# Linear attention's level products: each head alone on 64 rows, in two tiles of the scores' pool

## The chip, the cores and the metric

The kernel runs on one core of a Trainium2 chip. A core has five engines that work side by side, each through a queue of its own: TensorE (PE, matrix products into PSUM; its weight loads are listed as PEld), VectorE (DVE), ScalarE (ACT), GpSimd (POOL) and SyncE (SP, which issues the DMAs). The metric is the device time of one execution in microseconds, the median over runs.

## The reference

One step of a one-layer decoder. A 2048-token prompt and a small batch of 8 x 8 sample tokens go through an RMS norm and one input projection, whose columns feed two mixers: dilated sliding-window attention (8 heads of 64) and gated linear attention (GLA, 4 heads with key dimension 64 and value dimension 128). Both are gated, concatenated, projected and added to the input. What the change touches is GLA's scores within a chunk:

```python
b = jnp.cumsum(gc, axis=2)
diff = b[:, :, :, None, :] - b[:, :, None, :, :]
decay = jnp.exp(jnp.where(causal[:, :, None], diff, -jnp.inf))
scores = jnp.einsum('bhtk,bhsk,bhtsk->bhts', qc, kc, decay)
o = (jnp.einsum('bhts,bhsv->bhtv', scores, vc)
     + jnp.einsum('bhtk,bhkv->bhtv', qc * jnp.exp(b), state))
```

The score of query t with key s is a sum over 64 key dimensions, each with its own decay exp(b_t - b_s), for s not after t, separately for each head h.

## The kernel before

**Levels.** The decay has a factor per key dimension, so the scores aren't one matrix product. The kernel builds the lower triangle from levels. At level B (1, 2, 4, ..., 64) the tokens are cut into blocks of B; within each pair of blocks the left one gives keys and the right one queries, and the decay is split at the block border: exp(b_t - b_m) on the query, exp(b_m - b_s) on the key, both at most 1. One product per level then gives the scores of all such pairs, and a mask picks the part that belongs to them. The diagonal is set apart. A `gla_core` object works on 256 tokens (two chunks of 128): eight such objects (e0 to e7) for the prompt, and one small one (smp, three levels) for the samples.

**Where heads lie.** Keys and queries are turned so that the key dimension lies on the 128 partitions: a pair p of heads (two of the four) shares them, head j = 0 on partitions 0 to 63 and j = 1 on 64 to 127. Pairs and tokens lie along the row.

**`front(li)`** prepares a level. POOL subtracts the border's b (L236, tile D). ACT takes the exponential into E in three instructions (L244): the keys' half for all partitions into E[0], the queries' half of partitions 0 to 63 into E[1], and of 64 to 127 into E[2]. The other halves of E[1] and E[2] stay zero from a fill at the start (the loop at L1246, memset at L1252). DVE multiplies the keys into ks (L249, 128x256) and the queries into qbd (L252, 128x512): both blocks of qbd hold the same queries, but one has zeros on partitions 64 to 127, the other on 0 to 63. So a product over all 128 partitions gives two heads side by side with nothing of the one in the other.

**`back(li)`** makes the scores. A tile of the scores' pool ps_S (two buffers of one PSUM bank each) takes the products (L281): for each chunk c, head pair p and half k0 of the chunk's keys, one of 128 contracted partitions, 64 key columns as weights and 2 x 32 queries. That makes 8 products a level; each fp32 product runs as two passes, so the profile counts 16 matmuls. The first half of the keys goes to partitions 0 to 63 of the scores, the second to 64 to 127. DVE then copies the masked part into Ac (L287, copy_predicated). Level 64 (L267) has only keys of the first half: 4 products of 2 x 64 queries, all on partitions 0 to 63, copied by ACT into `full` (L273). `filled` copies Ac into `full` (L302).

**Order.** `gla_prompt` runs steps s = 0 to 8 for each core object e: front(s), then back(s - 2); `turned` and the two chunks of e - 1 at s = 0, 1 and 2 (`chunk`: U at L1275, the products with state and scores at L1283 and L1289, the state update Sbd at L1296 on DVE, the output copy on ACT); the next object's loads at s = 3, its `turn` and `decay` at 5 and 6. `weave` deals these steps out between the steps of the host, the input projections of g, vb and gb (L1127; 24 fp16 matmuls per 128 tokens and block, evicted by ACT), and beside them the weight preparation (`load_w`: ACT and DVE at L649 and L650), the dot products of the sample attention (`late_dots`: POOL at L1515, DVE at L970) and the sample's own linear attention (`sample_gla`). Each engine executes its instructions in the order in which they stand in its queue. That order is mostly the source's, but a planner lays it out with a timeline of its own and can put an instruction that is ready ahead of an earlier one that isn't.

After this stage the output projection follows (L1658), with the sample attention beside it.

Of the kernel before, what the change touches and what calls it, by code (L numbers as in the profile page):

```python
# [7 lines left out]
F32 = mybir.dt.float32  # L8
# [3 lines left out]
I32 = mybir.dt.int32  # L12
# [6 lines left out]
P = 128  # L19
# [33 lines left out]
def tile_hymba(ctx: ExitStack, tc: tile.TileContext, A: dict):  # L53
# [89 lines left out]
    class gla_core:  # L143
# [19 lines left out]
        def turn(self):  # L163
# [65 lines left out]
        def front(self, li):  # L229
            gt, st, n, B = self.pools[1], self.st, self.n, self.levels[li]  # L230
            halves = lambda f: f.rearrange("p (m two B) -> p m two B", two=2, B=B)
            M = n // B
            bv = halves(self.b[:].rearrange("p a c -> p (a c)"))
            D = gt.tile([P, 2 * n], F32, name=f"D_{self.tagp}_{B}", tag="D", bufs=2)
            dv = halves(D[:])
            dec = POOL.tensor_tensor(  # L236
                dv, bv, bv[:, :, 0:1, B - 1 : B].to_broadcast([P, M, 2, B]), ALU.subtract
            )
            E = st["E"][li % 2]
            ev = E[:, :, :n].rearrange("p i (m B) -> p i m B", B=B)  # L240
            for i, (rows, half) in enumerate(
                ((slice(0, P), 0), (slice(0, 64), 1), (slice(64, P), 1))
            ):
                ACT.activation(  # L244
                    ev[rows, i], dv[rows, :, half, :], AF.Exp, scale=(2 * half - 1) / 16.0
                )
            ks, qbd = st["ks"][li % 3], st["qbd"][li % 3]
            kv, qv = (halves(f.rearrange("p a c -> p (a c)")) for f in (self.kT, self.qT))
            DVE.tensor_tensor(  # L249
                halves(ks[:, : 2 * n])[:, :, 0, :], kv[:, :, 0, :], ev[:, 0], ALU.mult  # L250
            )
            que = DVE.tensor_tensor(  # L252
                qbd[:, :, :n].rearrange("p i (m B) -> p i m B", B=B),
                qv[:, :, 1, :].unsqueeze(1).to_broadcast([P, 2, M, B]), ev[:, 1:3], ALU.mult,
            )
            st["pins"] = (dec.ins, que.ins)

        def back(self, li):
            st, n, C, nch, B = self.st, self.n, self.C, self.nch, self.levels[li]
            ps_s, Ac = self.pools[3], self.Ac  # L260
            ks, qbd = st["ks"][li % 3], st["qbd"][li % 3]
            sc = ps_s.tile([P, 512], F32, name=f"sc_{self.tagp}_{B}", tag="S")
            if B == 64:

                for c in range(nch):
                    for p in range(2):
                        PE.matmul(  # L267
                            sc[:64, (c * 2 + p) * P : (c * 2 + p + 1) * P],
                            ks[:, p * n + c * C : p * n + c * C + 64],
                            qbd[:, :, (p * nch + c) * 64 : (p * nch + c + 1) * 64],  # L270
                            start=True, stop=True,
                        )
                ACT.activation(  # L273
                    self.full[0:64, :, 64:], sc[:64].rearrange("p (g t) -> p g t", t=64), AF.Copy
                )
                return
            for c in range(nch):
                for p in range(2):
                    o = (c * 2 + p) * 64
                    for k0 in range(0, C, 64):  # L280
                        PE.matmul(  # L281
                            sc[k0 : k0 + 64, o : o + 64],
                            ks[:, p * n + c * C + k0 : p * n + c * C + k0 + 64],
                            qbd[:, :, p * (n // 2) + (c * C + k0) // 2 :][:, :, :32],
                            start=True, stop=True,
                        )
            DVE.copy_predicated(  # L287
                Ac[:C].rearrange("p g (m two B) -> p g m two B", two=2, B=B)[:, :, :, 1, :],
                self.mask[:C, li].bitcast(I32).unsqueeze(1)
                .to_broadcast([C, nch * 4, 32]).rearrange("p g (m B) -> p g m B", B=B),  # L290
                sc[:C, : nch * 128].rearrange("p (g m B) -> p g m B", g=nch * 4, B=B),
            )
# [89 lines left out]
    with ExitStack() as c1:  # L382
# [862 lines left out]
        st = {"wgu": wgu, "E": [], "ks": [], "qbd": []}  # L1245
        for lst, nm_, shape, m, eng in (  # L1246
            (st["E"], "E", [P, 3, 256], 2, DVE), (st["ks"], "ks", [P, 512], 3, DVE),
            (st["qbd"], "qbd", [P, 2, 256], 3, DVE), (Sbd, "Sbd", [P, 2, 256], 2, POOL),
        ):
            for i in range(m):  # L1250
                t = gst.tile(shape, F32, name=f"{nm_}{i}")
                eng.memset(t[:], 0.0)  # L1252
# [14 lines left out]
        def chunk(core, gc):  # L1267
# [13 lines left out]
            for p in range(2):  # L1281
# [5 lines left out]
                for j in range(2):  # L1287
                    h = 2 * p + j
                    PE.matmul(  # L1289
                        O[:, h * P : (h + 1) * P], full[:, c * 4 + h, :],  # L1290
# [74 lines left out]
        def sample_gla():  # L1365
            while "dots" not in mixed:
# [13 lines left out]
            E, ks, qbd = (  # L1380
                own[:, 0:192].rearrange("p (i c) -> p i c", i=3), own[:, 192:320],
                own[:, 320:448].rearrange("p (i c) -> p i c", i=2),
            )
            own = {"wgu": wgu, "E": [E] * 2, "ks": [ks] * 3, "qbd": [qbd] * 3}
# [27 lines left out]
            for p in range(2):  # L1412
                O = ps_O.tile([P, 512], F32, name=f"O_s{p}", tag="O")
                for j in range(2):
# [8 lines left out]
                    for bt in range(8):  # L1423
# [5 lines left out]
                        O[:NS, j * P : (j + 1) * P], Am[:NS, h, :],  # L1429
# [606 lines left out]
```

## Time and profile before

| what | us |
|---|---|
| median of 3 runs | 1332.17 (1331.6 to 1335.26) |
| the profiled execution | 1337.86 |
| its span in the profile | 1336.1 |
| PE busy in the span | 1219.8 (91%) |
| DVE busy | 919.4 (69%) |
| ACT busy | 877.0 (66%) |
| POOL busy | 631.5 (47%) |
| mean granted TensorE clock | 0.974 |

The first level product of the prompt's linear attention starts at 744.6 us of the span, the last at 1022.2. All durations quoted below are from the one profiled execution. PE's busy time has modelled ends: a matmul's length contains the latency of the array, so the cost of a matmul in a stream is read from the distance of starts.

### The profile page before, as it was taken

What the parts mean: (1) busy time and instruction counts of PE and PEld (TensorE: products, weight loads), DVE (VectorE), ACT (ScalarE), POOL (GpSimd) and SP (SyncE); (2) the same over time, 40 slices, a digit from 0 to 9 for tenths busy, and PEclk for the clock granted to TensorE, in tenths of its full rate; (3) what the DMA queues carried; (4) which work ended last, traced back from release to release, by engine and by line L of the source; (5) the groups of instructions that cost most, each with busy time, mean ns of one, the idle gap of its engine ahead of it and who ended that gap; (6) DMA issues with size and microseconds to landing.
All of it is one profiled execution on the core that took longest, in us unless ns stands there. A gap on an engine that the chain in (4) does not pass through costs nothing.

```text
span 1336.1 us, 26268 instructions
## 1 busy us (share of the span) xinstructions
PE 1219.8 (91%) x8910; PEld 732.2 (55%) x8910; DVE 919.4 (69%) x2271; ACT 877.0 (66%) x2332; POOL 631.5 (47%) x596
## 2 busy tenths in 40 slices
PE   3797999989889898998999899999999989999998
PEld 1333565555555555676777566666655445444443
DVE  6357667788767876776765988777672388787741
ACT  5645787777668875878897667665774475565610
POOL 0067545678678745561113965665452144232310
PEclk9989999999999899999899999999999989999999
DMA  8859967777875599969886556553334788998952
GB/s 257 248 152 238 223 198 159 195 209 229 206 201 172 156 265 274 319 218 225 194 210 179 183 165 210 167 167 119 108 101 158 256 253 288 363 344 324 334 194 79
DMA packets 251800, 285.27 MB, mean 214 GB/s; under 512 B 125441, under 2 KB 160338, under 8 KB 251666
## 3 DMA queue, kind: packets, MB, share of 16 engines
q1 hardware_dynamic: 251666, 283.60, 70.7%
q8 instruction: 70, 1.15, 0.4%
q14 instruction: 64, 0.52, 0.1%
HBM read 183.12 MB, written 75.24 MB: 193 GB/s over the span
## 4 chain that ended last, share of the span: by engine, by line
PE 35%; DVE 19%; DMA 16%; issue 11%; ACT 9%; POOL 9%; SPq 2%; POOLq 0%; DVEq 0%; ACTq 0%
PE Y L1658 6%; PE acc_vb L1127 3%; DVE qbd L252 3%; PE acc_gb L1127 3%; PE acc_qkb L1127 3%; PE acc_g L1127 3%; POOL pr L965 2%; PE t L462 2%; PE O L477 2%; DMA T_q<-qp_d 2%; PE s L444 2%; DVE p L452 2%; DVE sck L970 2%; POOL pt L429 2%; DVE ks L249 1%
## 5 line engine op out<-in xcount | busy, mean ns | idle before, releaser
L1127 PEld LDWEIGHTS <-hr 128*128 128x128 f16 x1824 | 174.0, 99 | 133.9 <-issue 16.0
L1127 PEld LDWEIGHTS <-hl 128*128 128x128 f16 x1248 | 122.7, 100 | 154.9 <-issue 28.8
L455 ACT ACTIVATE p<-p,o 128x256 f32<-128x256 f32 (+1 forms) x384 | 173.3, 455 | 47.0 <-DVE o L452 39.8
L1658 PE MATMUL Y<-w_o,mh 128*128 128x512 f16 x768 | 178.0, 383 | 6.7 <-ACT mh L1617 6.6
L965 POOL TENSOR_TENSOR pr<-k,qb 128x512 f32<-128x512 f32 x96 | 132.5, 1380 | 91.8 <-DVE sck L970 58.6
L429 POOL TENSOR_TENSOR pt<-p,pt 128x512 f16<-128x512 f32 (+1 forms) x80 | 94.2, 1178 | 156.3 <-ACT pt L428 125.9
L477 PE MATMUL O<-v,pt 128*128 128x128 f16 x1200 | 113.1, 223 | 22.1 <-POOL pt L429 9.7
L1658 PEld LDWEIGHTS <-mh 128*128 128x128 f16 x768 | 71.9, 98 | 94.3 <-issue 9.0
L970 DVE TENSOR_REDUCE sck<-pr 128x8 f32<-128x512 f32 x128 | 85.6, 678 | 48.9 <-POOL pr L965 48.7
L462 PE MATMUL t<-ident,p 128*128 128x128 f32 x600 | 108.8, 286 | 7.3 <-ACT p L455 5.7
L477 PEld LDWEIGHTS <-pt 128*128 128x128 f16 x1200 | 83.7, 100 | 47.5 <-POOL pt L429 14.3
L1127 PE MATMUL acc_v<-w_v,hl 128*128 128x512 f16 x384 | 96.5, 396 | 8.8 <-DVE vp L759 3.1
L1127 PE MATMUL acc_g<-w_g,hr 128*128 128x272 f16 (+1 forms) x768 | 102.9, 280 | 0.0
L452 DVE CUSTOM_DVE_ANT_0 p<-s,m3w,scl_s 128x128 f32<-128x128 f32 (+1 forms) x256 | 89.0, 394 | 15.9 <-PE s L444 5.7
L1700 POOL TENSOR_TENSOR tc<-oc,w 128x512 f32<-128x512 f32 x32 | 47.0, 1490 | 111.7 <-DVE w L1692 104.8
L1127 PE MATMUL acc_q<-w_q,hl 128*128 128x512 f16 x384 | 93.8, 394 | 4.6 <-ACT zs_k L677 3.8
L244 ACT ACTIVATE E<-D_e 128x256 f32<-128x256 f32 x168 | 66.2, 417 | 43.8 <-POOL D_e L236 26.2
L1127 PE MATMUL acc_k<-w_k,hl 128*128 128x512 f16 x384 | 90.4, 381 | 3.1 <-ACT zs_k L677 2.6
L1127 PE MATMUL acc_vb<-w_vb,hr 128*128 128x512 f16 x384 | 89.1, 379 | 2.3 <-ACT zg L733 2.3
L444 PE MATMUL s<-kk,qq 128*128 128x256 f16 (+1 forms) x512 | 82.4, 273 | 8.9 <-DMA kk<-kp_d 5.2
L1127 PE MATMUL acc_gb<-w_gb,hr 128*128 128x512 f16 x384 | 87.7, 381 | 0.0
L462 PEld LDWEIGHTS t<-ident,p 128*128 128x128 f32 x600 | 70.3, 146 | 18.1 <-ACT p L455 11.3
(509 smaller groups left out, 2630.4 us busy)
## 6 DMA issues: line engine op xcount, KB each, us to landing
k<-in_cache_k_win SPq DMA_DIRECT2D x104, 256.0 KB
sv<-in_cache_v_win SPq DMA_DIRECT2D x24, 1024.0 KB
hr<-h_d SPq DMA_DIRECT2D x44, 512.0 KB
qb<-q_d SPq DMA_DIRECT2D x64, 256.0 KB
o_d<-o SPq DMA_DIRECT2D x96, 132.0 KB
oc<-o_d SPq DMA_DIRECT2D x48, 264.0 KB
x<-in_x_prompt SPq DMA_DIRECT2D x16, 512.0 KB
h_d<-hl SPq DMA_DIRECT2D x16, 512.0 KB
```

Source lines behind the costliest of these rows:

```text
L244: ACT.activation(ev[rows, i], dv[rows, :, half, :], AF.Exp, scale=(2 * half - 1) / 16.0)
L429: POOL.tensor_tensor(l, f, h, ALU.subtract)
L444: PE.matmul(s_ps[:, i * w : (i + 1) * w], q, k, start=(n == 0), stop=(n == len(prods) - 1),)
L452: DVE.tensor_tensor_reduce(s[:, sl], s_ps[:, sl], mask, neg, BIG, ALU.add, ALU.min, nmf(i))
L455: ACT.activation(s[:, sl], s[:, sl], AF.Exp, bias=nmf(i), scale=-1.0, accum_out=denf(i))
L462: PE.transpose(p_ps[:, i * P : (i + 1) * P], t["s"][:, i * P : (i + 1) * P], ident[:])
L477: PE.matmul(o_, t["pt"][:, c, (i * nb + b) * P : (i * nb + b + 1) * P], vf(i, b), start=(n == 0), stop=(n == 2 * nb - 1),)
L965: POOL.tensor_tensor(pr[:], kt, qt, ALU.mult)
L970: DVE.tensor_reduce(out, pr[:].rearrange("p (u k d) -> p u k d", u=2, k=4), AX.X, ALU.add)
L1127: PE.matmul(z, a_[:, k, :], w[:, p_, k, cols], start=(k == 0 and i == 0), stop=(k == KT - 1 and i == 2),)
L1658: PE.matmul(Y[:], a_[:, k, :], w_[:, part, k, :512], start=(i == 0), stop=(i == len(prods) - 1),)
L1700: eng.tensor_tensor(t_[:], oc[:, g, :, 0:64], w[:, g].unsqueeze(2).to_broadcast([P, NH, HD]), ALU.mult,)
```

## The change

The level products are made for each head alone. The queries qs are 128x256 with no zero blocks (E has two parts, and ACT takes the queries' exponential in one instruction). Each product contracts the 64 partitions of one head, and its result goes to a tile of that head's place j: `sc` is now two tiles of ps_S, so a level takes both buffers of the pool. There are 16 products of 32 queries a level (32 matmuls in the profile's count) and 8 of 64 at level 64. The masked copy into Ac and the copy of level 64 into `full` run once per tile. The heads in Ac and `full` are now ordered (j, c, p), in place of (c, p, j), which the diagonal (POOL) and the readers of `full` and Ac follow. Fills of E and of the queries are dropped.

```diff
 in turn():
+            g = nch * 2
             POOL.tensor_tensor(
-                Ac[:C],
-                ident64[:C].unsqueeze(1).to_broadcast([C, nch * 4, 64]),
-                dd[:C].unsqueeze(2).to_broadcast([C, nch * 4, 64]),
+                Ac[:C].rearrange("p (j g) t -> p j g t", j=2),
+                ident64[:C].unsqueeze(1).unsqueeze(1).to_broadcast([C, 2, g, 64]),
+                dd[:C].rearrange("p (g j) -> p j g", j=2).unsqueeze(3).to_broadcast([C, 2, g, 64]),
                 ALU.mult,
             )
 in front():
-            for i, (rows, half) in enumerate(
-                ((slice(0, P), 0), (slice(0, 64), 1), (slice(64, P), 1))
-            ):
+            for half in range(2):
                 ACT.activation(
-                    ev[rows, i], dv[rows, :, half, :], AF.Exp, scale=(2 * half - 1) / 16.0
+                    ev[:, half], dv[:, :, half, :], AF.Exp, scale=(2 * half - 1) / 16.0
                 )
...
             que = DVE.tensor_tensor(
-                qbd[:, :, :n].rearrange("p i (m B) -> p i m B", B=B),
-                qv[:, :, 1, :].unsqueeze(1).to_broadcast([P, 2, M, B]), ev[:, 1:3], ALU.mult,
+                qs[:, :n].rearrange("p (m B) -> p m B", B=B), qv[:, :, 1, :], ev[:, 1], ALU.mult
             )
 in back():
-            sc = ps_s.tile([P, 512], F32, name=f"sc_{self.tagp}_{B}", tag="S")
+            sc = [
+                ps_s.tile([P, 512], F32, name=f"sc_{self.tagp}_{B}_{j}", tag="S") for j in range(2)
+            ]
+            heads = (slice(0, 64), slice(64, P))
...
-                        PE.matmul(
-                            sc[k0 : k0 + 64, o : o + 64],
-                            ks[:, p * n + c * C + k0 : p * n + c * C + k0 + 64],
-                            qbd[:, :, p * (n // 2) + (c * C + k0) // 2 :][:, :, :32],
-                            start=True, stop=True,
-                        )
-            DVE.copy_predicated(
-                Ac[:C].rearrange("p g (m two B) -> p g m two B", two=2, B=B)[:, :, :, 1, :],
-...
-            )
+                        for j, rows in enumerate(heads):
+                            PE.matmul(
+                                sc[j][k0 : k0 + 64, o : o + 32],
+                                ks[rows, p * n + c * C + k0 : p * n + c * C + k0 + 64],
+                                qs[rows, p * (n // 2) + (c * C + k0) // 2 :][:, :32],
+                                start=True, stop=True,
+                            )
+            G = nch * 2
+            for j in range(2):
+                DVE.copy_predicated(
+                    Ac[:C, j * G : j * G + G].rearrange("p g (m two B) -> p g m two B", two=2, B=B)[
+                        :, :, :, 1, :
+                    ],
+...
+                )
 in tile_hymba():
-            (st["E"], "E", [P, 3, 256], 2, DVE), (st["ks"], "ks", [P, 512], 3, DVE),
-            (st["qbd"], "qbd", [P, 2, 256], 3, DVE), (Sbd, "Sbd", [P, 2, 256], 2, POOL),
+            (st["E"], "E", [P, 2, 256], 2, None), (st["ks"], "ks", [P, 512], 3, DVE),
+            (st["qs"], "qs", [P, 256], 3, None), (Sbd, "Sbd", [P, 2, 256], 2, POOL),
...
-                        O[:, h * P : (h + 1) * P], full[:, c * 4 + h, :],
+                        O[:, h * P : (h + 1) * P], full[:, 4 * j + 2 * c + p, :],
```

Level 64 is split in the same way: its products go per head to the first 64 partitions of the two tiles, in columns 0 to 255, and two ACT copies of 64x256 bring them into `full`. The sample's `gla_core` uses the same code with tiles of its own.

More of the change, by code (lines that the diff above doesn't have):

```diff
@@ L266, in back @@
                     for p in range(2):
[L267 to L270, printed above, removed]
-                            start=True, stop=True,
-                        )
-                ACT.activation(
-                    self.full[0:64, :, 64:], sc[:64].rearrange("p (g t) -> p g t", t=64), AF.Copy
-                )
+                        g = c * 2 + p
+                        for j, rows in enumerate(heads):
+                            PE.matmul(
+                                sc[j][:64, g * 64 : g * 64 + 64],
+                                ks[rows, p * n + c * C : p * n + c * C + 64],
+                                qs[rows, (p * nch + c) * 64 : (p * nch + c + 1) * 64],
+                                start=True, stop=True,
+                            )
+                for j in range(2):
+                    ACT.activation(
+                        self.full[0:64, 4 * j : 4 * j + 4, 64:],
+                        sc[j][:64, 0:256].rearrange("p (g t) -> p g t", t=64), AF.Copy,
+                    )
                 return
@@ L278, in back @@
                 for p in range(2):
[L279 removed]
+                    o = (c * 2 + p) * 32
                     for k0 in range(0, C, 64):
[L281 to L292 removed]
+                        for j, rows in enumerate(heads):
+                            PE.matmul(
+                                sc[j][k0 : k0 + 64, o : o + 32],
+                                ks[rows, p * n + c * C + k0 : p * n + c * C + k0 + 64],
+                                qs[rows, p * (n // 2) + (c * C + k0) // 2 :][:, :32],
+                                start=True, stop=True,
+                            )
+            G = nch * 2
+            for j in range(2):
+                DVE.copy_predicated(
+                    Ac[:C, j * G : j * G + G].rearrange("p g (m two B) -> p g m two B", two=2, B=B)[
+                        :, :, :, 1, :
+                    ],
+                    self.mask[:C, li].bitcast(I32).unsqueeze(1)
+                    .to_broadcast([C, G, 32]).rearrange("p g (m B) -> p g m B", B=B),
+                    sc[j][:C, : G * 32].rearrange("p (g m B) -> p g m B", g=G, B=B),
+                )
         def queries(self):
@@ L1379, in sample_gla @@
             DVE.memset(own[:], 0.0)
[L1380 to L1382 removed]
+            E, ks, qs = (
+                own[:, 0:128].rearrange("p (i c) -> p i c", i=2), own[:, 128:256], own[:, 256:320]
             )
[L1384 removed]
+            own = {"wgu": wgu, "E": [E] * 2, "ks": [ks] * 3, "qs": [qs] * 3}
             core = gla_core(
```

11 lines of the change are left out of this document (6 added, 5 removed).

## The prediction

> **What bounds the kernel now.** I read the page's first line, for the span, and then cut the linear-attention stage (740 to 1016 us) into stretches of 40 us and read each engine's busy time in them.
>
> ```profile
> span 1336.1 us, 26268 instructions
> ```
> ```profile
> 740.00:780.00 40.00, 34.25 (x338) 24.48 (x336) 38.24 (x48) 26.49 (x70) 36.32 (x29) 0.96 0.57 182
> ...
> 820.00:860.00 40.00, 39.23 (x357) 27.20 (x356) 32.43 (x52) 24.13 (x64) 23.28 (x19) 1.00 0.65 207
> 860.00:900.00 40.00, 39.57 (x358) 27.89 (x357) 28.69 (x43) 25.07 (x65) 26.34 (x22) 1.00 0.53 164
> ```
>
> The columns of the second fence are the stretch, its length, and the busy time of PE, PEld, DVE, ACT and POOL. From 820 to 900 PE lacks under 1 us in each 40 us, while DVE falls from 32 to 29. Only from 740 to 780 is DVE the full one (38.24), and there PE loses 5.75 us. The stage runs at PE's pace: work taken from DVE and ACT can bring back only the time in which PE stands still, and any change of PE's own work counts in full. What is measured below one per cent must therefore be worked out from PE's stream.
>
> Next I read PE's timeline in the quiet part, to learn what one matmul costs PE there (columns: start, length, what, count), and the tile of the level products, sc_e, with min/median/max ns.
>
> ```profile
> 862.58 0.69 PE L281 MATMUL sc_e<-qbd,ks 128*64 128x64 f32 x16
> 863.20 1.83 PE L1127 MATMUL acc_g<-w_g,hr 128*128 128x272 f16 x15
> 864.96 1.09 PE L267 MATMUL sc_e<-qbd,ks 128*64 128x128 f32 x8
> 865.98 1.48 PE L1127 MATMUL acc_g<-w_g,hr 128*128 128x256 f16 x12
> ...
> 879.17 0.61 PE L1289 MATMUL O<-vb,full 128*128 128x128 f32 x4
> 879.62 0.60 PE L1283 MATMUL O<-Sbd,qe_e 128*128 128x256 f32 x2
> ```
> ```profile
> L281 PEld LDWEIGHTS sc_e<-qbd,ks x768: 132/138/139, 744.6 to 1015.2; 128*64 128x64 f32 x192
> L281 PE MATMUL sc_e<-qbd,ks x768: 219/222/272, 744.6 to 1015.3; 128*64 128x64 f32 x192
> ...
> L273 ACT ACTIVATE full<-sc_e x8: 572/582/592, 766.8 to 1022.5; 64x512 f32<-64x512 f32 x8
> ```
>
> A group's length ends with the latency of its last matmul, so the cost of one comes from starts. An fp32 product of 128 columns on the whole array costs 0.11 us (four from 879.17 to 879.62): 0.87 ns a column. The 16 level matmuls (8 products, two passes each) of 64 columns would take 16 x 64 x 0.87 = 0.89 us in a row, but from 862.58 to the next instruction pass 0.62 us. With the latency of 0.22 off (the median of L281's matmul), the starts fill 0.69 - 0.22 = 0.47 us, or 0.058 us per pair: the two products of a pair fill different output halves (rows 0-63 and 64-127 of the scores) and run side by side. The other 0.62 - 0.47 - 0.06 = 0.09 us is lost in changing over to the host's matmuls. The last level (L267) writes rows 0-63 alone: 8 of 128 columns take 1.02 us, 8 x 0.11 plus the changes, nothing side by side.
>
> Last, the rows of the same timeline in which PE stood still before a GLA instruction, or beside one:
>
> ```profile
> 746.14 0.69 PE L281 MATMUL sc_e<-qbd,ks 128*64 128x64 f32 x16 [0.89 <-DVE qbd L252]
> ...
> 752.00 0.69 PE L281 MATMUL sc_e<-qbd,ks 128*64 128x64 f32 x16 [1.45 <-DVE qbd L252]
> ...
> 763.19 1.79 PE L267 MATMUL sc_e<-qbd,ks 128*64 128x128 f32 x8 [2.09 <-DVE Ac_e L287]
> ...
> 771.98 0.69 PE L281 MATMUL sc_e<-qbd,ks 128*64 128x64 f32 x16 [0.41 <-DVE qbd L252]
> 773.23 0.66 PE L1275 MATMUL U<-vb,kdt_e 128*64 128x128 f32 x8 [0.56 <-DVE Sbd L1296]
> ...
> 816.59 4.69 PE L1127 MATMUL acc_vb<-w_vb,hr 128*128 128x512 f16 x21 [2.35 <-ACT zg L733]
> ...
> 843.08 0.66 PE L1275 MATMUL U<-vb,kdt_e 128*64 128x128 f32 x8 [0.77 <-DVE Sbd L1296]
> ...
> 878.05 0.66 PE L1275 MATMUL U<-vb,kdt_e 128*64 128x128 f32 x8 [0.43 <-DVE Sbd L1296]
> ...
> 913.10 0.66 PE L1275 MATMUL U<-vb,kdt_e 128*64 128x128 f32 x8 [0.76 <-DVE Sbd L1296]
> ```
>
> The brackets hold the idle time and who ended it. On the level chain in DVE: 0.89 + 1.45 + 2.09 + 0.41 = 4.84 us. On the state update (Sbd) for U: 0.56 + 0.77 + 0.43 + 0.76 = 2.52 us. On ACT: 2.35 us. That is about all that a faster DVE and ACT can give: under 10 us.
>
> **The change part by part.**
>
> ```profile
> L252 DVE TENSOR_TENSOR qbd<-kq_e,E 128x512 f32<-128x512 f32 x56 | 71.1, 1269 | 0.5 <-ACT E L244 0.4
> ...
> L244 ACT ACTIVATE E<-D_e 64x256 f32<-64x256 f32 x112 | 46.5, 416 | 8.9 <-DVE qbd L252 7.3
> L249 DVE TENSOR_TENSOR ks<-kq_e,E 128x256 f32<-128x256 f32 x56 | 40.7, 727 | 17.6 <-ACT E L244 9.8 <-PE sc_e L281 5.9 <-PE acc_g L1127 1.6
> ```
> ```profile
> L287 DVE COPY_PREDICATED Ac_e<-gmask,sc_e x48: 415/436/743, 749.1 to 1015.5; 128x256 f32<-128x256 int32 x48
> ...
> L287 DVE COPY_PREDICATED Ac_smp<-gmask,sc_smp x3: 271/407/424, 976.2 to 988.1; 64x128 f32<-64x128 int32 x3
> ```
>
> DVE: the query product (L252) shrinks from 128x512 to 128x256, the form of ks (L249). By that row 56 x (1269 - 727) = 30 us less. The copy of each level becomes two of half size; by the shortest of each form (271 ns with 128 elements a row, 415 with 256) two cost 0.54 against 0.42, 48 x 0.13 = 6 us more. The fills of E and qbd fall away before the first level. Net some 24 us, none of it on PE. ACT: one of three exponentials goes, 56 x 0.416 = 23 us less. The last level's copy into full becomes two, which by the 416 ns of 64x256 cost 0.83 against the 0.58 of L273 above, 2 us more. The diagonal on POOL (L177) keeps its element count, in another order of heads, and nothing but its readers changes; cost nothing, since from 820 to 900 POOL is busy 26 of 40 us at most, and 8 us if each of 8 took a microsecond more.
>
> PE: every level product is cut in four quarters of the array: 64 rows of one head, 64 output rows. So 32 matmuls of 32 columns and 32 weight loads of 64 columns stand in place of 16 and 16. What they cost hangs on the loads. The sample branch's scores (L1821) have narrower ones:
>
> ```profile
> L1821 PEld LDWEIGHTS R<-ksT,qx x64: 106/110/111, 1105.0 to 1234.7; 128*32 128x32 f32 x64
> L1821 PE MATMUL R<-ksT,qx x64: 218/219/244, 1105.0 to 1234.8; 128*32 128x64 f32 x64
> ```
> ```profile
> 1104.97 0.43 PE L1821 MATMUL R<-ksT,qx 128*32 128x64 f32 x16
> 1105.33 1.04 PE L1658 MATMUL Y<-w_o,mh 128*128 128x512 f16 x4
> ```
>
> A load of 32 columns takes 110 ns and one of 64 (L281) takes 138: 28 ns for 32 columns, so 56 ns of streaming for a load of 64. Now 16 such loads hide under 0.53 us of matmuls, which they could not in a row (0.90): loads of the two output halves already overlap. The sample scores show four strips at once: 16 matmuls of 64 columns start within 0.43 - 0.22 = 0.21 us, four per 0.055 us. In the changed kernel each quarter gets 8 loads x 56 = 0.45 us and 8 matmuls x 28 = 0.22 us under them. If the four quarters run side by side, a level takes 0.45 to 0.47 us as now: **0**. No row of this trace has matmuls on the upper and lower 64 input rows at once, so I keep both ends. Best: loads cost nothing, 0.22 against 0.47, 48 x -0.25 = -12 us. Worst: the two input halves take turns, 0.90 against 0.45, with three sample levels 51 x 0.45 = +23 us. I take 0, because strips of the output side do run side by side in both rows, for loads and matmuls alike, and I know no reason here why input halves should not.
>
> Here a rule of the Trainium skill speaks against the change. TensorEngine Tiling (Array Packing), Instruction Overhead, says that each matmul has some 60 cycles of overhead, that one column lasts as long as 60, and that one should not take the tiling from a dimension that is already small. By it 32 columns would cost what 64 do, and the sum would be that of the first rival below. The trace speaks against a floor per instruction: 16 matmuls in 0.21 us is 13 ns from start to start.
>
> The last level goes from 8 matmuls of 128 columns in a row (0.88 us) to 16 of 64 in two input halves: 8 x 56 = 0.45 us. 8 x -0.43 = **-3.4 us**; 0 if the halves take turns. In seven steps a burst stands right ahead of U, whose tiles have 128 input rows; a changeover at 0.09 us each: **+0.6 us**.
>
> Stalls: in the first forty microseconds DVE is full, and a level there loses some 0.4 us of DVE work (0.54 - 0.13). Half of the 4.84 us of level stalls: **-2.4 us** (0 to -4.8). U waits for Sbd, which stands on DVE behind the query products of the steps before it, two of which are 0.5 us shorter: three quarters of 2.52, **-1.9 us** (0 to -2.5). The 2.35 us behind zg stand beside the weight preparation of w_gb, which stays: 0.
>
> **The wait that is added.** The scores' pool has two buffers. Now a level takes one, so the products of level l+1 can start while the copy of level l is outstanding. After, a level takes both, and its first products wait until both copies of the level before it are done. Behind a waiting product stand the host's projections, since PE takes its queue in order, and then whoever reads the accumulators (ACT's evictions).
>
> ```profile
> 749.10 0.72 DVE L287 COPY_PREDICATED Ac_e<-gmask,sc_e 128x256 f32<-128x256 int32 x1
> ...
> 775.78 0.74 DVE L287 COPY_PREDICATED Ac_e<-gmask,sc_e 128x256 f32<-128x256 int32 x1
> ...
> 813.90 5.69 DVE L650 SCALAR_TENSOR_TENSOR w_gb<-wr_gb,ns_gb,w_gb 128x512 f16<-128x512 f32 x5
> 819.61 0.73 DVE L287 COPY_PREDICATED Ac_e<-gmask,sc_e 128x256 f32<-128x256 int32 x1
> ...
> 859.44 0.42 DVE L287 COPY_PREDICATED Ac_e<-gmask,sc_e 128x256 f32<-128x256 int32 x1 [2.54 <-PE sc_e L281]
> ```
> ```profile
> 801.13 0.70 PE L1283 MATMUL O<-Sbd,qe_e 128*128 128x256 f32 x2
> 801.76 0.38 PE L582 MATMUL mx_gb<-mm_gb,ident 1*128 1x1 f32 x2
> 802.07 0.71 PE L1289 MATMUL O<-vb,full 128*128 128x128 f32 x4
> ...
> 812.47 0.69 PE L281 MATMUL sc_e<-qbd,ks 128*64 128x64 f32 x16
> ```
>
> In the quiet part this costs nothing: the copy from 859.44 was over at 859.86, and the next burst starts at 862.58 (above). In the first three pairs of chunks they are late. The burst at 746.14 started 3.7 us before the first copy's end (749.10 + 0.72), the burst at 771.98 4.5 us before 776.52, the burst at 812.47 7.9 us before 820.34, behind five pieces of w_gb. In the last case PE stands 2.35 us anyway, so 5.5 would be new. Together 13.7 us if order and times stay. They won't quite: the shorter DVE work brings copies forward, and the instruction order on each engine is laid out by a planner, which puts independent work ahead: at 801.76 a weight maximum stands in the middle of a chunk's products, which the source emits in one piece. I take **+2 us** (0 to 13.7).
>
> **Sum.** 0 - 3.4 + 0.6 - 2.4 - 1.9 + 2 = -5.1 us. The profiled execution took 1337.86 us (its span of 1336.1 and 1.8 us around it); with the change 1332.8. The median of the runs, 1332.17, is 0.43% below the profiled one, so the forecast is 1332.8 x 1332.17 / 1337.86 = **1327 us**, 0.4% faster. A measurement of this kernel tells about 0.3% (4 us) from no change.
>
> **The rivals.** *Input halves take turns.* PE then pays 51 x 0.45 = 23 us more, the last level gains nothing: 23 + 0.6 - 2.4 - 1.9 + 2 = +21 us, 1353 us on the median's scale. For it: no row shows input halves at once. Against it: output strips overlap fully. It turns slower from 0.1 us per level on. The Trainium skill's rule quoted above would end at this price too. *One buffer in effect.* The added wait stands at its full 13.7 us in the three places above: +6.6 us, 1339 us. For it: three bursts really ran ahead of their copies, and w_gb's pieces come from loads and ACT, whose times no order can fix ahead. Against it: from 843 on there is room, and PE has other work that can be put first. It turns slower when the waits add up to more than 7 us. *Nothing to see.* PE's stage is full, the relief on DVE and ACT falls where nobody waits, and the new waits eat the last level's 3.4 us: 1332 us. For it: only 7 of 276 us are stalls that DVE causes.
>
> **How the numbers follow.** The forecast's case has 0.60: with its own spread of some 5 us either way (1332 down to 1317; wholly free loads would give 1315), 0.40 faster, 0.18 within the bound, 0.02 slower. Turns: 0.18, all slower. One buffer: 0.12, of it 0.11 slower. Nothing to see: 0.10, of it 0.09 within. Sums: faster 0.41, same 0.28, slower 0.31. The range reaches from 1317 to 1347: it takes in the one-buffer case and leaves out nearly all of the turns case (0.16) and a little below.
>
> **What would show it.** Right: level products x1536 with starts of four in some 0.06 us, a burst of 32 no longer than 0.7 us; the last level's group at half its 0.82 us of starts; the query product near 0.7 us; U without its 0.4 to 0.8 us. Wrong: bursts of 1.1 us (turns); idle of PE before level products ended by the copies at L287's place in the first three pairs (one buffer); or a planner's order so different that the host's matmuls themselves wait, which no row here can exclude.

## The result: 0.6% slower, and the profile after

| | before | changed |
|---|---|---|
| median of 11 runs each | 1334.54 us (1329.73 to 1337.24) | 1341.5 us (1336.68 to 1345.58) |
| ratio, 95% interval | | 1.0058 [1.0043, 1.0074] |
| profiled execution, span | 1336.1 us | 1336.5 us |

The forecast was 1327 us and faster; the kernel became about 8 us slower. The two profiled executions differ by 0.4 us only: that of before lies at the upper end of its runs, that of the changed kernel at the lower end of its own. So I compare traces from a point up to which both do the same, the last product of the projection acc_qkb, to the last product of the output stage, Y. In the tile views the last two times are the first and the last start:

```profile
L1127 PE MATMUL acc_qkb<-w_qkb,hr x288: 378/379/635, 505.0 to 621.7; 128*128 128x512 f16 x144
...
L1658 PE MATMUL Y<-w_o,mh x768: 378/379/635, 1090.0 to 1331.2; 128*128 128x512 f16 x192
```
```profile
L1137 PE MATMUL acc_qkb<-w_qkb,hr x288: 379/379/634, 500.9 to 617.7; 128*128 128x512 f16 x144
...
L1668 PE MATMUL Y<-w_o,mh x768: 376/379/634, 1088.2 to 1331.6; 128*128 128x512 f16 x192
```

First fence before, second changed: 1331.2 - 621.7 = 709.5 us against 713.9, 4.4 us more. This stretch is the measure in what follows. It comes from one execution, and in the table of the experiments it differs from what the ratios give by up to 5 us.

PE has less to do than before, and stands still more. In the stretch it is idle for 41.4 us, against 37.2 before: that is nearly the whole difference. The page of the changed kernel, then its stretches of 40 us (columns as in the prediction; behind POOL's stands the granted TensorE clock):

```profile
span 1336.5 us, 27968 instructions
...
PE 1215.3 (91%) x9754; PEld 726.4 (54%) x9754; DVE 899.3 (67%) x2317; ACT 849.7 (64%) x2281; POOL 615.6 (46%) x596
```
```profile
740.00:780.00 40.00, 37.09 (x401) 24.32 (x400) 35.17 (x50) 21.77 (x53) 33.69 (x30) 0.91 0.51 165
780.00:820.00 40.00, 36.56 (x461) 26.15 (x458) 34.81 (x65) 23.86 (x64) 24.38 (x22) 1.00 0.65 202
820.00:860.00 40.00, 35.76 (x439) 25.72 (x440) 30.10 (x52) 20.85 (x64) 24.78 (x22) 0.96 0.58 174
860.00:900.00 40.00, 39.30 (x499) 27.35 (x497) 29.48 (x56) 21.82 (x67) 26.05 (x23) 1.00 0.53 164
```

From 740 to 780 PE is busier than before (37.09 against 34.25), as hoped. From 820 to 860 it lost 4 us where it had lost under 1 (35.76 against 39.23), though DVE, ACT and POOL have room there. The granted clock in these two stretches is 0.91 and 0.96, against 0.96 and 1.00 before, so some of the busy time is slower work: by 0.05 x 40 up to 2 of the 2.8 us that PE is busier in the first.

PE's own work came out as the prediction drew it. PE's timeline of the changed kernel:

```profile
874.68 0.67 PE L287 MATMUL sc_e<-qs,ks 64*64 64x32 f32 x32
875.28 1.81 PE L1137 MATMUL acc_g<-w_g,hr 128*128 128x256 f16 x15
...
878.75 0.68 PE L270 MATMUL sc_e<-qs,ks 64*64 64x64 f32 x16
879.37 1.04 PE L1137 MATMUL acc_vb<-w_vb,hr 128*128 128x512 f16 x4
```
```profile
L287 PE MATMUL sc_e<-qs,ks x1536: 219/219/313, 746.7 to 1026.0; 64*64 64x32 f32 x192
...
L295 DVE COPY_PREDICATED Ac_e<-gmask,sc_e x96: 260/297/504, 751.1 to 1026.4; 128x128 f32<-128x128 int32 x96
```

A level takes 0.60 us to the next instruction (0.62 before), the last level 0.62 (1.02 before). But the second fence (the tile sc_e, a product and the copy that DVE makes of it) shows the chain of levels late: its last copy starts at 1026.4, which is 408.7 us after acc_qkb, against 1015.5 - 621.7 = 393.8 before. And this is where PE stood still in the stage:

```profile
751.58 0.95 PE L287 MATMUL sc_e<-qs,ks 64*64 64x32 f32 x32 [1.23 <-DVE Ac_e L295]
...
760.78 0.86 PE L287 MATMUL sc_e<-qs,ks 64*64 64x32 f32 x32 [0.69 <-DVE Ac_e L295]
...
798.13 0.66 PE L1286 MATMUL U<-vb,kdt_e 128*64 128x128 f32 x8 [1.61 <-DVE Sbd L1307]
...
821.23 0.70 PE L1294 MATMUL O<-Sbd,qe_e 128*128 128x256 f32 x2 [2.37 <-DVE Sbd L1307]
...
853.87 0.96 PE L1294 MATMUL O<-Sbd,qe_e 128*128 128x256 f32 x2 [3.01 <-DVE Sbd L1307]
...
896.67 0.86 PE L287 MATMUL sc_e<-qs,ks 64*64 64x32 f32 x32 [0.70 <-DVE Ac_e L295]
...
939.62 0.66 PE L1286 MATMUL U<-vb,kdt_e 128*64 128x128 f32 x8 [1.72 <-DVE kdt_e L336]
```

The level products wait for the copies of the level before, a little. The chunks' products do, for Sbd and kdt_e, and they wait longer than any did before. The largest gap of all stands at the start of the output stage (changed kernel first, then before):

```profile
1073.79 4.05 PE L1137 MATMUL acc_gb<-w_gb,hr 128*128 128x512 f16 x18
1085.85 1.03 PE L1626 MATMUL tm<-ident,mt 128*128 128x128 f16 x8 [8.01 <-ACT mt L1616]
```
```profile
1090.04 1.89 PE L1658 MATMUL Y<-w_o,mh 128*128 128x512 f16 x4 [4.55 <-ACT mh L1617]
```

PE waits 8.0 us there instead of 4.6. DVE's timeline says why (changed, then before):

```profile
1068.23 0.68 DVE L1477 TENSOR_TENSOR S<-S,U_s 128x512 f32<-128x512 f32 x1
...
1069.23 0.19 DVE L122 TENSOR_SCALAR rv_ob<-ob_ss 128x68 f32<-128x68 f32 x1
...
1075.00 0.69 DVE L1586 TENSOR_SCALAR zl_s<-zl_s 64x1024 f32<-64x1024 f32 x1 [5.32 <-DMA zl_s<-gb_d]
...
1078.50 0.74 DVE L1706 SCALAR_TENSOR_TENSOR mix<-obl,smx,zl 128x512 f32<-128x512 f32 x1
```
```profile
1049.92 0.20 DVE L122 TENSOR_SCALAR rv_ob<-ob_ss 128x68 f32<-128x68 f32 x1 [6.38 <-ACT obq_c L334]
...
1066.14 0.74 DVE L1696 SCALAR_TENSOR_TENSOR mix<-obl,smx,zl 128x512 f32<-128x512 f32 x1
```

Before, the rsqrt over all the sums of squares (rv_ob is its first step) ran as soon as the last of them was there, at 1050, and the first mix at 1066. In the changed kernel the planner set the rsqrt behind the sample branch's last state add, and behind it DVE waits 5.3 us for a load of the sample's gates. None of these lines is in the diff.

One more line moved that the diff doesn't touch. It is the load of the queries and keys for the first pair of chunks, in SyncE's queue (before, then changed):

```profile
L155 SPq DMA_DIRECT2D zqk_e<-zqk_d x8: 370/382/608, 600.7 to 894.0; - x8
```
```profile
L155 SPq DMA_DIRECT2D zqk_e<-zqk_d x8: 371/397/667, 726.2 to 889.1; - x8
```

The first of the eight loads is issued at 726 us instead of 601. The tiles' addresses in the built program explain it. E and the queries shrink by 5 KB a partition (2 x 1 + 3 x 1), and all pools behind them move down by as much. The first buffer of zqk began at byte 100480 of each partition, and now it begins at 95360. The output tiles o of the attention stage end at byte 97632, and in the changed kernel's trace the last of them is stored at 724.6:

```profile
L947 SPq DMA_DIRECT2D o_d<-o x14: 319/320/1226, 690.6 to 724.6; - x14
```

The load that could go some 125 us ahead now has to wait for them: it may not overwrite them before they are stored.

### The profile page after: what moved, and what is told of

It reads as the page before. It is cut to its first block, busy times and chain, and to the rows that moved or that the text cites. A ratio compares the mean times of both kernels' runs of the same rounds, so it can differ in the third digit from the quotient of the medians.

```text
span 1336.5 us, 27968 instructions
## 1 busy us (share of the span) xinstructions
PE 1215.3 (91%) x9754; PEld 726.4 (54%) x9754; DVE 899.3 (67%) x2317; ACT 849.7 (64%) x2281; POOL 615.6 (46%) x596
## 4 chain that ended last, share of the span: by engine, by line
PE 42%; DVE 17%; DMA 13%; issue 12%; POOL 9%; ACT 5%; SPq 2%; POOLq 0%; DVEq 0%; ACTq 0%
PE acc_gb L1137 5%; PE Y L1668 4%; PE acc_vb L1137 4%; PE acc_qkb L1137 4%; PE acc_q L1137 3%; PE acc_g L1137 3%; PE t L472 3%; PE s L454 3%; PE O L487 3%; PE acc_v L1137 2%; POOL pr L975 2%; PE acc_k L1137 2%; DMA T_q<-qp_d 2%; DVE ks L248 2%; DVE qs L251 2%
## 5 line engine op out<-in xcount | busy, mean ns | idle before, releaser
L465 ACT ACTIVATE p<-p,o 128x256 f32<-128x256 f32 (+1 forms) x384 | 173.4, 455 | 47.3 <-DVE o L462 40.6
L980 DVE TENSOR_REDUCE sck<-pr 128x8 f32<-128x512 f32 x128 | 85.7, 680 | 48.5 <-POOL pr L975 48.3
L1710 POOL TENSOR_TENSOR tc<-oc,w 128x512 f32<-128x512 f32 x32 | 44.2, 1401 | 134.6 <-DVE w L1702 96.4
L1137 PE MATMUL acc_vb<-w_vb,hr 128*128 128x512 f16 x384 | 92.0, 379 | 0.0
L237 POOL TENSOR_TENSOR D_e<-b_e 128x512 f32<-128x512 f32 x56 | 61.0, 1094 | 58.5 <-ACT E L243 45.6
L243 ACT ACTIVATE E<-D_e 128x256 f32<-128x256 f32 x112 | 43.7, 417 | 60.8 <-DVE ks L248 34.6
```

Of the source, the lines that this page charges most:

```text
L237: dec = POOL.tensor_tensor(dv, bv, bv[:, :, 0:1, B - 1 : B].to_broadcast([P, M, 2, B]), ALU.subtract)
L465: ACT.activation(s[:, sl], s[:, sl], AF.Exp, bias=nmf(i), scale=-1.0, accum_out=denf(i))
L980: DVE.tensor_reduce(out, pr[:].rearrange("p (u k d) -> p u k d", u=2, k=4), AX.X, ALU.add)
L1137: PE.matmul(z, a_[:, k, :], w[:, p_, k, cols], start=(k == 0 and i == 0), stop=(k == KT - 1 and i == 2),)
L1710: eng.tensor_tensor(t_[:], oc[:, g, :, 0:64], w[:, g].unsqueeze(2).to_broadcast([P, NH, HD]), ALU.mult,)
```

## The experiments

I had two theories. **W**: the wait that the prediction priced at 2 us is dearer, because a level takes both buffers of the scores' pool and the levels wait for each other. **M**: the memory that moved throws the order of work about, at the end of the stage or at its start. Every ratio is to the kernel before, with its 95% interval; the last columns are the first issue of a zqk load, the time of the rsqrt, the stretch from acc_qkb to the last Y, and PE's idle time in that stretch, all in us from the profiled execution.

| kernel | ratio | zqk | rsqrt | stretch | idle |
|---|---|---|---|---|---|
| before | 1 | 600.7 | 1049.9 | 709.5 | 37.2 |
| changed | 1.0058 [1.0043, 1.0074] | 726.2 | 1069.2 | 713.9 | 41.4 |
| e1_pad | 0.9971 [0.9953, 0.9990] | 597.1 | 1042.7 | 707.7 | 37.0 |
| e6_pad3k | 0.9998 [0.9982, 1.0013] | 600.3 | 1044.9 | 707.7 | 36.6 |
| e12_tables | 1.0006 [0.9985, 1.0026] | 598.9 | 1067.2 | 707.6 | 38.5 |
| e5_padshift | 1.0028 [1.0005, 1.0051] | 600.1 | 1069.7 | 711.9 | 40.5 |
| e6_pad2k | 1.0058 [1.0037, 1.0080] | 730.0 | 1053.5 | 714.0 | 41.1 |
| e11_fullgc | 1.0053 [1.0032, 1.0075] | 726.9 | 1049.8 | 711.4 | 41.2 |
| e3_shift | 1.0018 [0.9997, 1.0038] | 599.5 | 1071.1 | 707.5 | 36.1 |
| e8_split | 0.9994 [0.9979, 1.0010] | 599.1 | 1049.6 | 710.0 | 37.8 |
| e2_pair | 0.9924 [0.9901, 0.9948] | 598.7 | 1040.2 | 698.8 | 30.6 |
| e10_rev | 0.9941 [0.9920, 0.9962] | 596.0 | 1039.8 | 703.4 | 32.2 |
| e9_wide | 1.0041 [1.0021, 1.0061] | 597.9 | 1049.0 | 711.9 | 38.1 |
| e4_borrow_pad | 1.0172 [1.0144, 1.0200] | 599.6 | 1067.0 | 729.1 | 38.2 |

### The memory alone put right

```diff
+old_shape = {"E": [P, 3, 256], "qs": [P, 2, 256]}
-t = gst.tile(shape, F32, name=f"{nm_}{i}")
+t = gst.tile(old_shape.get(nm_, shape), F32, name=f"{nm_}{i}")
...
-lst.append(t)
+lst.append(t[:, 0, :] if nm_ == "qs" else t[:, 0:2, :] if nm_ == "E" else t)
```

> The changed kernel with E and the queries allocated in their old sizes ([P, 3, 256] and [P, 2, 256], the spare parts never touched), so that every later tile lies where it lay before the change. Theory M (the smaller tiles move the memory of the output stage over other tiles, the planner then puts the rsqrt of ob_ss behind the sample's last state add, and PE idles at the start of the output stage): rsqrt back before 1055 us, first mix before 1070, PE idle before the first tm 4 to 5 us instead of 8.0, time 5 to 6 us below the changed kernel (about 1336, ratio 1.000 to 1.002 to the kernel before). Theory W (a level takes both buffers of the scores' pool, levels wait for each other, and that costs the time): tail as it comes, time within 2 us of the changed kernel (ratio 1.004 to 1.006).

0.9971: the whole loss is gone, and a little more. The rsqrt is back at 1042.7, the first zqk load at 597. W, which expected no difference, falls here. M is right that it is the memory, but the 5 to 6 us that it took for the end alone are too few: by the ratios 0.9% or 12 us came back.

### The wait for both buffers alone

```diff
-sc = ps_s.tile([P, 512], F32, name=f"sc_{self.tagp}_{B}", tag="S")
+sc = [
+    ps_s.tile([P, 512], F32, name=f"sc_{self.tagp}_{B}_{c}", tag="S") for c in range(nch)
+]
...
-sc[k0 : k0 + 64, o : o + 64],
+sc[c][k0 : k0 + 64, p * 64 : p * 64 + 64],
...
+for c in range(nch):
+    DVE.copy_predicated(...)
```

> The kernel before with one part of the change alone: each level's scores lie in two tiles of the scores' pool, here one for each chunk of 128 rows, with two copies; products on 128 rows with zero blocks as before, memory as before. Theory W: levels wait for each other as in the changed kernel (POOL's wait of D for ACT E near 45 us instead of 5, DVE's wait of Ac for sc near 30 instead of 17) and the time is 5 to 9 us over the kernel before (ratio 1.004 to 1.007), more than in the changed kernel, which has PE's gain against it. Theory M: the same waits, but the chunks' work is not late at the end (U_s last at 1067 us in both kernels), so 0 to 3 us (ratio 1.000 to 1.002).

0.9924, ten microseconds faster: both theories missed. Three more kernels ask about this. e8_split has only the split copies, in one tile:

> The kernel before with the split copies of e2_pair alone: a level's scores in one tile of the pool, the copies of the chunks of 128 rows in two instructions. If e2_pair's 10 us come from the copies (the second half's products run while the first half is copied, shorter DVE instructions between the others), ratio 0.992 to 0.995 as there. If they come from the pool (levels held back, the projections put ahead of them, 8.8 us of PE idle at the level products becoming 2.2), ratio 0.999 to 1.002.

0.9994: nothing from the copies. e10_rev is e2_pair with the chunks of a level in the other order:

> e2_pair with the two chunks of a level in the other order (chunk 1's products and copy first); the same instructions, sizes, memory and pool, so only the planner's order differs. Theory 'both buffers held': e2_pair's gain is due to the pool and stays (ratio 0.990 to 0.995). Theory 'luck of the order': any such swap moves the time by some 5 to 10 us, and e2_pair was a lucky one: ratio 0.997 or more.

0.9941: the gain survives another order. So it is the second tile, with which a level holds both buffers of the pool: it made this kernel some 0.6 to 0.8% faster. (The second tile also puts the two chunks in two banks; no kernel here tells that apart.) PE's idle time in the stretch falls from 37.2 us (37.8 in e8_split) to 30.6 and 32.2; at the level products it falls from 8.8 us to 2.2 in e2_pair (gaps after a level product, added up over the trace). A likely reading, not tested by itself, is that the planner sets host projections where a level would have to wait. And the opposite, the changed kernel with e1_pad's memory and one of the two tiles from the projections' pool, so that two levels can be in flight:

```diff
-ps_s.tile([P, 512], F32, name=f"sc_{self.tagp}_{B}_{j}", tag="S") for j in range(2)
+(ps_s, self.pools[4])[j].tile(
+    [P, 512], F32, name=f"sc_{self.tagp}_{B}_{j}", tag=("S", "PT")[j]
+) for j in range(2)
```

> The changed kernel with the old sizes of allocation as in e1_pad, and the second head's tile of a level from the projections' pool ps_P (tag PT, two buffers) instead of the scores' pool, so that two levels can be in flight again. Theory W: POOL's wait of D for ACT E back near 5 us, time 5 to 7 us under the kernel before (about 1328, ratio 0.995 to 0.996), since PE's gain of the prediction is then left. Theory M alone: as e1_pad, within 2 us (ratio 0.999 to 1.002).

1.0172, far slower. PE's timeline of e4_borrow_pad shows a level cut up:

```profile
871.12 0.42 PE L289 MATMUL sc_e<-qs,ks 64*64 64x32 f32 x8
871.47 1.09 PE L196 MATMUL ptg_e<-ident,zqk_e 128*128 128x128 f32 x8
872.49 0.42 PE L289 MATMUL sc_e<-qs,ks 64*64 64x32 f32 x8
872.84 0.87 PE L1139 MATMUL acc_g<-w_g,hr 128*128 128x272 f16 x6
```

Eight matmuls cost 0.35 us to the next instruction, 32 in one piece 0.60. The level products stand in 94 pieces instead of 56 in the changed kernel, and PE's time for them, gaps left out, is 52.4 us instead of 35.2. PE is idle for 38.2 us of the stretch, hardly more than in e1_pad (37.0), so these 17 us of work, and not waits, are most of the 21 us by which the stretch is longer. What the projections lose with one buffer of their pool was not told apart from it.

### Which memory: the end or the start

e3_shift gives the kernel before the end of the changed one, with 5 KB left free under the output stage's pools:

```diff
+room = c1.enter_context(tc.tile_pool(name="room", bufs=1))
+room.tile([P, 1280], F32, name="room")
 cb = c1.enter_context(tc.tile_pool(name="cb", bufs=2, reuse_waits="tile"))
```

> The kernel before with 5 KB a partition left free at the base of the output stage's pools, so that they lie over the GLA stage's tiles as in the changed kernel; nothing else. Theory M: rsqrt of ob_ss behind the sample's last state add (1065 us or later instead of 1050), PE idle before the first tm 7 to 9 us, time 4 to 6 us over the kernel before (ratio 1.003 to 1.0045). Theory W: the time of the kernel before (ratio within 0.0015 of 1).

The order of the end came as expected (rsqrt at 1071.1), the price didn't: 1.0018, not clear of 1 and outside the ranges of both theories. By it the end's order costs the old kernel some 2 us, by its interval 5 at most. In the trace PE waits 4.4 + 1.9 us for the first mixed tiles, where it waited 4.6 before. e5_padshift does the same in e1_pad:

> The changed kernel with E and the queries in their old allocation (as e1_pad) and 5 KB left free at the base of the output stage's pools (as e3_shift): the GLA stage's memory lies as before the change, the output stage lies over it as in the changed kernel. The load of the first zqk is expected near 600 us again (it was 597 in e1_pad, 726 in the changed kernel) and the rsqrt of ob_ss behind the sample's last state add, as in the changed kernel. Theory 'end': what e1_pad won over the changed kernel (11 us by the ratios 1.0058 and 0.9971) is all the output stage's late start, so this kernel comes out near 1341 (ratio 1.004 to 1.006). Theory 'start and end add up': the end costs what e3_shift showed, 2 to 5 us, so near 1335 (ratio 0.998 to 1.001). Theory 'start': near e1_pad (ratio 0.996 to 0.998).

1.0028, so 0.3 to 0.6% over e1_pad and e6_pad3k: some of the loss, not all, and in none of the three ranges. Its mirror lets the end be and leaves the start wrong by 224 bytes:

```diff
+gst.tile([P, 512], F32, name="room")
 Sbd = []
```

> The changed kernel with a tile of 2 KB at the head of the GLA stage's memory, so that it lies 3 KB lower than before the change and not 5: the first zqk still touches the last 224 bytes of an attention output tile, and its load comes after 720 us; the rsqrt of ob_ss comes before the sample's last adds again. The mirror of e5_padshift. Theory 'end': near e1_pad (1332, ratio 0.996 to 0.998). Theory 'start and end add up': 6 to 9 us over e1_pad (ratio 1.001 to 1.004). Theory 'start': as the changed kernel (ratio 1.004 to 1.006).

> The changed kernel with a tile of 3 KB at the head of the GLA stage's memory: 1 KB more than in e6_pad2k, enough to clear the attention output tiles, so the first zqk loads near 600 us; the end as in e1_pad. All theories of the start and the end: e1_pad within 0.002 (ratio 0.995 to 0.999), though E, ks, qs and all later tiles lie 2 KB from where they lie there. The rival 'any shift of the memory throws the planner's order about, and 5 to 10 us with it': more than 4 us from e1_pad on either side.

One kilobyte stands between these two (512 and 768 elements). The tile zqk_e in SyncE's queue, e6_pad2k first:

```profile
L155 SPq DMA_DIRECT2D zqk_e<-zqk_d x8: 371/396/614, 730.0 to 892.8; - x8
```
```profile
L155 SPq DMA_DIRECT2D zqk_e<-zqk_d x8: 370/376/610, 600.3 to 894.5; - x8
```

1.0058 against 0.9998: the kilobyte that makes this load late brings the whole loss of the changed kernel, with the rsqrt in time. Up to the end of the linear attention PE waits in e6_pad2k as in the changed kernel, at the same products and as long; what follows differs, and e6_pad2k loses time in the output stage, with one wait of 5.9 us for a load of the value cache (2.9 in e6_pad3k).

e6_pad3k is 0.0027 from e1_pad (0.9971), more than the 0.002 expected and less than the 4 us of the rival, a mere scatter by any shift. The traces settle it: though the tiles lie 2 KB apart, PE, DVE, ACT and POOL execute the same instructions in the same order in both, from end to end, while the orders of e6_pad2k and e6_pad3k part at some 725 us, where the first zqk is used. A shift by itself doesn't throw the order about. It also follows that two measurements of one order can differ by 0.3%, and nothing smaller in the table should be read.

Then the same in the kernel before, where only the tile full changes its pool, which lowers zqk by 4 KB:

```diff
-full = gst.tile([P, 8, P], F32, name="full")
+full = gc.tile([P, 8, P], F32, name="full")
```

> The kernel before with the tile full taken from the last pool of the GLA stage (gc) instead of the first (gst), nothing else: gst ends 4 KB lower, so that the first zqk lies on attention output tiles as it does in the changed kernel, while the pools behind gc and the output stage lie as they did. Theory 'start': the first zqk loads after 720 us, the first level products start some 128 us after the last product of acc_qkb instead of 123, and the old products lose by it too, 4 to 8 us (ratio 1.003 to 1.006). Rival 'only with the new products': a late load costs only where the planner's order comes out badly; ratio within 0.0015 of 1.

1.0053 with no line of arithmetic changed: as much as the whole change cost. Its stretch is 711.4 us, 1.9 more than before, so its profiled execution shows only a part of that; PE is idle for 4.0 us more, and new waits stand at the level products (1.5, 2.4 and 2.6 us for copies). And the changed kernel with its three tables moved from gc to gst, which raises zqk without spare bytes:

> The changed kernel with its three tables (masks, scan_m, wgu; 2.9 KB) taken from gst instead of gc, so that the first zqk clears the attention output tiles without a spare byte: the first zqk loads near 600 us, the rsqrt of ob_ss still comes behind the sample's last adds. Start put right, end not, as in e5_padshift by another way. Theory 'start and end': as e5_padshift (1.0028), 1.001 to 1.005; theory 'start alone': as e1_pad and e6_pad3k, 0.996 to 1.000; 'luck of the order': outside both.

1.0006, between the ranges of the theories, with the load at 599 and the rsqrt late. Its first level products are late all the same (747.9, 128 us after acc_qkb; 129 in the changed kernel, 123 in e1_pad), so a late first level is not what costs; the loss goes with the late load. All three kernels that have it lose 0.5 to 0.6%, and PE is idle for 41.1 to 41.4 us in their stretches, against 36.6 to 38.5 in e1_pad, e6_pad3k and e12_tables. How the late load brings the loss about is **open**: the planner lays out another order from there on, the three traces lose the time in three different places, and no kernel here has the late load with the old order.

### What the products cost

e9_wide has the changed products on the old front (three exponentials, blocks with zeros, fills, memory):

```diff
-qs[rows, p * (n // 2) + (c * C + k0) // 2 :][:, :32],
+qbd[rows, j, p * (n // 2) + (c * C + k0) // 2 :][:, :32],
```

> The kernel before with the changed kernel's products alone: row halves of 64, two tiles of the scores' pool by head, two copies; but the exponentials in three instructions, the queries multiplied into blocks with zeros (which the products no longer read), the fills and the memory as before the change. Asks what keeps the changed kernel with its memory put right (e1_pad 0.9971, e6_pad3k 0.9998) from e2_pair's 0.9924, though its level products take 3.6 us less of PE. Theory 'products': the products or the copies by head lose it; near e6_pad3k (ratio 0.996 to 1.000). Theory 'short front': the shorter ACT and DVE instructions let the planner put the next levels' multiplies ahead of the state updates, for which PE then waits 3.0 and 2.6 us; near e2_pair or under it (ratio 0.989 to 0.993).

1.0041, over the ranges of both theories, against 0.9924 and 0.9941 for the old products in two tiles: the products or the copies by head lose 1%, although PE spends 36.1 us on them (gaps left out) against 38.9 in e2_pair. The theory of the short front falls: with it (e1_pad, e6_pad3k) the kernel is 0.4 to 0.7% faster than e9_wide. PE's waits in e9_wide stand at the chunks:

```profile
756.08 0.66 PE L337 MATMUL ptk_e<-ident,kd_e 128*128 128x128 f32 x4 [2.30 <-POOL kd_e L329]
...
783.28 0.70 PE L1296 MATMUL O<-Sbd,qe_e 128*128 128x256 f32 x2 [2.30 <-ACT ob_c L343]
...
835.75 1.11 PE L337 MATMUL ptk_e<-ident,kd_e 128*128 128x128 f32 x4 [2.45 <-POOL kd_e L329]
```

Why the planner lays the chunks' work worse beside 32 products by head than beside 16 by chunk is **open**. A kernel of row halves with tiles by chunk would tell it, but there two row halves would write to one bank at once. The Trainium skill, TensorEngine Tiling (Array Packing), Restrictions and Gotchas, says that different row tiles cannot access the same PSUM bank at the same time; no run here shows it.

**The sum of the parts**, in ratios to before: both buffers held, 0.9932 (mean of e2_pair and e10_rev); products by row halves and head, up to 1.0041; the short front, down to 0.9985 (mean of e1_pad and e6_pad3k); the memory, up to 1.0058. Four steps of -0.7, +1.1, -0.6 and +0.7%, each uncertain by some 0.3%. The change with its memory put right is no slower than before; e2_pair beats both kernels.

## The prediction, step by step

- **Level products, 0 (-12 to +23): right for PE itself** (what e9_wide lost stands in waits of other products). A full level went from 0.618 us to 0.600 (median from first start to next instruction). The quarters of the array run side by side, and *Input halves take turns* is refuted. The Trainium skill's rule that was weighed against the change (TensorEngine Tiling (Array Packing), Instruction Overhead) didn't bring its price either: 32 matmuls of 32 columns start within 0.45 us, 14 ns apart. That speaks against a floor for each matmul in turn; each quarter had 8 of them in that time, so a floor within a quarter stays untested.
- **Last level, -3.4: right.** 8 x (1.019 - 0.614) = -3.2. All level products together, gaps left out, went from 40.6 to 35.2 us: these two, and fewer pieces (56 for 62).
- **Changeovers ahead of U, +0.6: open.** A burst right ahead of U costs the changed kernel 0.60 us, as much as ahead of any other product; before, most such bursts ran into a wait, so there is no clean figure to set beside it.
- **Stalls of levels, -2.4, and the added wait, +2: right, the first at the end of its range.** Of the 4.84 us on DVE's level chain none is left in its old places. Waits for the copies stand there now, 1.23, 0.69 and 0.70 us in the rows above: 2.6 us. That is the sign the prediction named for *One buffer in effect*, at a fifth of that rival's 13.7. So it is chance that the measured 1341.5 us lies near this rival's 1339, and inside the range.
- **DVE's relief: smaller than reckoned.** The groups of the changed kernel by line, within the stage:

```profile
L251 DVE TENSOR_TENSOR qs<-kq_e,E 128x256 f32<-128x256 f32 x56 | 48.3, 862 | 0.0
```

The query product takes 862 ns instead of the 727 expected, so 71.1 - 48.3 = 23 us less and not 30.
- **The stall behind zg, 0: off to the good side.** The 2.35 us at 816.59 have no counterpart.
- **U's waits for Sbd, -1.9: wrong.** The waits for Sbd, at U and now at O, grew: 1.61 + 2.37 + 3.01 = 7.0 us against 2.5, and up to 1.7 us a time for kdt_e came in. The prediction took DVE's order as given and shortened it; the planner made another. Its list of waits also ended at 915 us. It lacks 1.20 us for Sbd at 948.02 and 2.63 us for a weight maximum on DVE at 987.93 of the kernel before, so that DVE's stalls were 11 of 276 us and not 7; the changed kernel has neither.
- **The step that failed:** the smaller tiles, costed at nothing. Of E and the queries the prediction counted the fills that fall away, "before the first level". It did not ask what lies on the 5 KB that become free, nor what moves down. That moved a load by 126 us and the end's rsqrt by 19, and cost 0.7% (0.9985 to 1.0058). The sum of -5.1 us, 0.4%, stands against 0.9971 and 0.9998 with the memory put right: of the right sign, and their mean (0.9985) is four tenths of the size. Even that is partly luck, since two effects that the prediction didn't price, -0.7% from the second tile and +1.1% from products and copies by head, stand against each other in it.
- **The added wait's side effect had the wrong sign.** Holding both buffers was priced at 0 to 13.7 us lost; alone it is a gain of some 9.
- The third sign of being wrong, "a planner's order so different that the host's matmuls themselves wait", comes nearest to the trace, though it is the chunks' products (4 us between 820 and 860) and the output stage's first ones (8.0 us) that wait. It had no rival and no chance of its own, so that a slower kernel could come only from prices in the level's own neighbourhood.

## What to carry to other kernels

A tile that becomes smaller moves every tile behind it. Before such a change is priced, look up which older tiles the moved ones come to lie on and how long those are in use; compare the first issue of each load before and after. Where a planner lays out the order, test a change once with the old sizes kept as padding, to tell the change from the move. And a buffer more in flight is not always better: in e4_borrow_pad the planner cut the level products into more pieces, and on PE each piece had its price.

## What the runs showed of the hardware

Many stalls repeat to some 0.01 us where the order is the same: the changed kernel and e6_pad2k both have 2.37 and 3.01 us at O, e1_pad and e6_pad3k both have 3.00 and 2.56 us for Sbd. Not all do: a wait for kdt_e is 1.45 us in e1_pad and 0.55 in e6_pad3k.

The 3.01 us have a curious cause. DVE's and POOL's timelines of the changed kernel:

```profile
847.47 5.38 DVE L248 TENSOR_TENSOR ks<-kq_e,E 128x256 f32<-128x256 f32 x1
852.77 0.41 DVE L251 TENSOR_TENSOR qs<-kq_e,E 128x256 f32<-128x256 f32 x1
853.11 0.70 DVE L1307 SCALAR_TENSOR_TENSOR Sbd<-Sbd,eb_e,U 64x128 f32<-64x128 f32 x2
```
```profile
847.85 1.05 POOL L237 TENSOR_TENSOR D_e<-b_e 128x512 f32<-128x512 f32 x1
848.87 2.48 POOL L1525 TENSOR_TENSOR pr<-k,qb 128x512 f32<-128x512 f32 x2
851.32 1.25 POOL L326 TENSOR_TENSOR kd_e<-kd_e,kq_e 128x512 f32<-128x512 f32 x1
854.30 1.05 POOL L237 TENSOR_TENSOR D_e<-b_e 128x512 f32<-128x512 f32 x1 [1.73 <-ACT E L243]
```

A product whose shortest case takes 0.39 us took 5.38, and ended 0.3 us after POOL's unbroken run of four instructions did (851.32 + 1.25 = 852.57). The same product took 5.38 us beside the same run in e6_pad2k. The Trainium skill, Trainium Architecture — The Big Picture, What this means for kernel authors, says that DVE and GpSimd share a pair of ports under an exclusive lock. The trace fits that, and adds that a run of POOL instructions without a gap can keep one DVE instruction waiting through all of them. It was read from the trace, not tested by itself.
